# A two-layer hybrid encoder on one core: GpSimd's tensor work goes to the vector and scalar engines, and the MLP norm's factor, squared, goes into the last residual add

## The chip, the cores and the metric

One Trainium2 chip, one of its cores. The metric is the device time of one execution in microseconds (us). The engines go by their short names: PE is the tensor engine (matmul), PEld its weight loads, DVE the vector engine, ACT the scalar engine, POOL GpSimd, SP the engine that issues the DMAs.

## The reference, cut to what matters

The program runs two layers over 256 tokens of 1024 features in float32. Each layer normalises, projects to many branches (a gated linear attention, a dilated attention, a differential attention, a "hyena" convolution by Fourier transform), merges them by gates, projects out, and ends with an MLP:

```
for i in range(2):
    h = rmsnorm(x, norm1_g[i])
    ...
    x = x + m @ w_out[i]
    h2 = rmsnorm(x, norm2_g[i])
    x = x + square(relu(h2 @ mlp_w1[i])) @ mlp_w2[i]

rmsnorm(x, g) = x * rsqrt(mean(x*x) + 1e-6) * g
hyena: y = irfft(rfft(z) * rfft(kern)); kern from two filters hf, hb over the sum of their absolute values
       return x0 * (y + z * skip)
```

The factor rsqrt(...) of a token is one positive number r. It passes through the matrix product and the ReLU unchanged, and comes out of the square as r squared, so it may as well be multiplied in at the end, token by token.

## The kernel before, in words

**Tiling.** The 256 tokens are two blocks of 128 (tb 0 and 1). Every float32 factor of a large product is split into a high part `hi` and a remainder `lo`, and each product is three matmuls (`mm3`, lines 241 to 243: hi by hi, hi by lo, lo by hi). Weights come as `raw` tiles by DMA from SP; `split_to` (line 210 on) makes their `hi` on ACT (line 222) and their `lo = raw - hi` on DVE (line 224), up to four halves of a unit ahead of use. Products whose output has tokens on the partitions go through `chunk_tm`: 128x512 matmuls into two PSUM tiles, one for each token block, either with the blocks side by side or, with `tb_major`, first all of block 0 and then all of block 1. `hooks={(tb, q): f}` calls `f` ahead of quarter `q` of block `tb`. Products with features on the partitions go through `unit_fm` with 128x256 matmuls.

**What POOL does.** While `self.relief` is set, `split_to` gives every second `lo` to POOL (line 223). It is set at three kinds of places: before the first layer's input projections, in `out_proj` when half of the `wo1` product is done, and in the last products of an MLP that another layer follows. POOL also does the four sums of the hyena filters (lines 572 to 581), four of the twelve products and sums that multiply two spectra, and the difference PO of the two results (lines 900 to 907), and it scales z by the skip gain (line 914). Besides, it does the reciprocal root of every norm (`rstd`, lines 302 and 303: an add, then a power of -0.5), on 1 to 8 numbers of each partition.

**Order of the work.** The attention and hyena branches are generators. `tick` runs between groups of matmuls. It lets every generator in `evq` take one step, and one in `mixq` if the credit (1.4 for a tick, up to 3.0) is positive; what a step yields is taken off the credit. So the numbers that a generator yields place its matmuls among the large products. All engines run their instructions in the order written.

**Around the change.** `out_proj` runs `wo0` (output columns 0 to 511), then `wo1` (columns 512 to 1023, `tb_major`). After each, `residual` adds PSUM to x on DVE (line 359) and `square` sums x squared on ACT (line 355). `norm_scale(tb)` takes the sum on POOL (line 364), `rstd` on POOL, and makes `xn = x * r * g` in two halves on DVE (line 375), with g broadcast to all partitions by a 512 KB load. `norm_trans(tb)` transposes xn on PE (line 310) and splits the result into `hi` on ACT (line 317) and `lo` on DVE (line 318), tile name `act`. The first product of the MLP, `m1b` (also `tb_major`), needs these. For block 0 both are hooked into `wo1`'s second half; for block 1 `norm_scale` follows `wo1` and `norm_trans` is hooked into `m1b`.

Of the kernel before, what the change touches and what calls it, by code (L numbers as in the profile page):

```python
# [14 lines left out]
ALU = mybir.AluOpType  # L15
# [106 lines left out]
class Kern:  # L122
    def __init__(self, ctx, tc, a):
# [17 lines left out]
        self.evq, self.mixq = [], []  # L141
        self.relief = False
        self.credit = 0.0
# [198 lines left out]

    def load_gain(self, g=None):
        self.gt = None
        if g is not None:
            t = self.t4([128, D], "g")
# [9 lines left out]

    def residual(self, tb, c, p, o=0, n=512):
        xs = self.x[tb][:, c * 512 + o:c * 512 + o + n]
        self.nc.vector.tensor_add(xs, xs, p)

# [15 lines left out]

    def norm_trans(self, tb):
        t = slice(tb * 128, tb * 128 + 128)
        for c in range(2):
            p = self.transposes([self.xn[c][:, j * 128:(j + 1) * 128] for j in range(4)])  # L380
            hi, lo = [self.hpair[i][c][:, :, t] for i in range(2)]
            if self.gt is not None:
                self.split(hi, lo, p)
                continue
            gs = [self.gcol[:, 4 * c + j:4 * c + j + 1] for j in range(4)]
            for j in range(4):
                self.nc.scalar.activation(hi[:, j].bitcast(F32R), p[:, j], AF.Identity, scale=gs[j])
            for j in range(4):
                self.nc.vector.scalar_tensor_tensor(lo[:, j].bitcast(F32R), p[:, j], gs[j], hi[:, j], ALU.mult, ALU.subtract)

# [6 lines left out]
    def setup(self):  # L397
# [133 lines left out]
    def filters(self, p):  # L531
# [43 lines left out]
        ab = [self.t4([128, 2, 512], "ab") for _ in range(2)]  # L575
        nc.scalar.activation(ab[0], hf, AF.Abs)
        nc.scalar.activation(ab[1], hb, AF.Abs)
        yield 0.0
        nc.gpsimd.tensor_add(ab[0], ab[0], ab[1])
        yield 0.0  # L580
        nc.gpsimd.tensor_add(ab[0][:, 0], ab[0][:, 0], ab[0][:, 1])
        p.K = [self.t4([128, 2, 512], "K") for _ in range(2)]
# [11 lines left out]
        for cb in range(4):  # L594
            nc.tensor.matmul(ps[:, cb:cb + 1], lhsT=ab[0][:, 0, cb * 128:(cb + 1) * 128], rhs=self.one, start=True, stop=True)
        p.invn = self.cp.tile([128, 4], F32, tag=f"invn{l}", name=self.nm("invn"))
# [6 lines left out]
    def gla_in(self, act, p):  # L603
# [8 lines left out]
        self.chunk_tm("gr", act, ev_r, tb_major=True, hooks={(1, 0) if self.l else (0, 3): lambda: self.norm_trans(1)})  # L612
        self.relief = False
        st.v1, lr = self.t2([128, 2, 256], "dv1"), self.t2([128, 2, 32], "lr")
# [257 lines left out]
    def hyena(self, st, p):  # L872
# [177 lines left out]

    def out_proj(self, gain):
        act = self.views(self.mpair)
        self.load_gain(gain)

# [8 lines left out]
        def mid():  # L1063
            self.relief = True
            self.norm_scale(0)

        self.chunk_tm("wo1", act, ev(1), tb_major=True, hooks={(1, 0): mid, (1, 3): lambda: self.norm_trans(0)})
        self.norm_scale(1)
        return self.views(self.hpair)

    def mlp(self, act, last):
# [16 lines left out]
        def first():  # L1088
# [18 lines left out]
            g = []  # L1107
            self.chunk_tm("m1b", act, ev, tb_major=True, hooks={(1, 0): lambda: self.norm_trans(1)})
            self.relief = False
            for j in range(2):  # L1110
# [23 lines left out]
        ws = [self.take(f"m2.{j}", k, ahead=False) for j in (14, 15) for k in range(2)]  # L1134
        self.relief = not last
        for tb in range(2):
            for c in range(2):
# [6 lines left out]
                if last:  # L1144
                    n = 256 if tb and c else 512
                    for o in range(0, 512, n):
                        self.residual(tb, c, acc[tb][c][:, o:o + n], o, n)
                        cc = slice(c * 512 + o, c * 512 + o + n)
                        nc.sync.dma_start(self.a["out"][tb * 128:(tb + 1) * 128, cc], self.x[tb][:, cc])
                elif tb == 0:  # L1150
                    self.residual(tb, c, acc[tb][c])
                    self.square(tb, c)
            if tb == 0 and not last:
                self.norm_scale(0)
        if not last:
            for c in range(2):
                self.residual(1, c, acc[1][c])
                self.square(1, c)
            self.norm_scale(1)

    def run(self):
# [11 lines left out]
        self.norm_scale(1)  # L1173
        self.relief = True
        p = self.params(0)
        self.evq += [p.derive, self.filters(p)]
        for l in range(L):
# [67 lines left out]
def lay_out(inputs):  # L1245
# [11 lines left out]
    for l in range(L):  # L1257
# [10 lines left out]
        for i, k in enumerate(("hy_b1", "hy_freq1", "hy_b2", "hy_freq2")):  # L1268
# [28 lines left out]
```

## Time and profile before

| | |
|---|---|
| time, median of 3 runs | 1133.13 us (1133.01 to 1134.49) |
| the profiled execution: own time | 1133.93 us |
| the profiled execution: span from first to last instruction | 1132.1 us |
| busy: PE, DVE, ACT, POOL | 97%, 65%, 51%, 14% of the span |
| granted clock of PE, mean | 0.990 |
| DMA | 196.87 MB, mean 174 GB/s |

Times in the trace count from the first instruction. A matmul's shown duration is modelled and overlaps the next; how fast PE runs is read from the distance between starts. Idle time of an engine stands in brackets behind a row, with what ended it.

### The profile page before, as it was taken

What the parts mean: (1) busy time and instruction counts of PE and PEld (TensorE: products, weight loads), DVE (VectorE), ACT (ScalarE), POOL (GpSimd) and SP (SyncE); (2) the same over time, 40 slices, a digit from 0 to 9 for tenths busy, and PEclk for the clock granted to TensorE, in tenths of its full rate; (3) what the DMA queues carried; (4) which work ended last, traced back from release to release, by engine and by line L of the source; (5) the groups of instructions that cost most, each with busy time, mean ns of one, the idle gap of its engine ahead of it and who ended that gap; (6) DMA issues with size and microseconds to landing.
All of it is one profiled execution on the core that took longest, in us unless ns stands there. A gap on an engine that the chain in (4) does not pass through costs nothing. (4 is left out here: it accounts for less than half of the span.)

```text
span 1132.1 us, 17927 instructions
## 1 busy us (share of the span) xinstructions
PE 1100.9 (97%) x7374; PEld 983.4 (87%) x7374; DVE 734.5 (65%) x993; ACT 575.3 (51%) x870; POOL 156.5 (14%) x124
## 2 busy tenths in 40 slices
PE   7999989999999899999999999899999998999998
PEld 5889778999999688899878997789999996989997
DVE  5787776658567667755555777676486665555644
ACT  6854535555444356444547555445463454454542
POOL 2031362000000210300030014530010003100000
PEclk9999999999999999999999999999999998999999
DMA  8434445743464554445435444366534653545452
GB/s 306 174 134 150 167 150 157 216 165 134 150 223 172 190 198 179 166 177 223 156 135 217 149 159 158 145 177 184 202 112 149 223 205 112 217 160 218 180 192 75
DMA packets 41527, 196.87 MB, mean 174 GB/s; under 512 B 4770, under 2 KB 15939, under 8 KB 20197
## 3 DMA queue, kind: packets, MB, share of 16 engines
q1 hardware_dynamic: 41444, 195.72, 48.9%
q8 instruction: 58, 0.95, 0.3%
q14 instruction: 25, 0.20, 0.1%
HBM read 194.62 MB, written 1.08 MB: 173 GB/s over the span
## 5 line engine op out<-in xcount | busy, mean ns | idle before, releaser
L224 DVE TENSOR_TENSOR lo<-raw,hi 128x1024 fp32r<-128x1024 f32 x338 | 423.4, 1272 | 132.6 <-ACT hi L222 132.0
L241 PE MATMUL w<-act,hi 128*128 128x256 f32 x1440 | 407.1, 283 | 0.0
L242 PE MATMUL w<-act,hi 128*128 128x256 f32 x1440 | 401.1, 279 | 0.0
L243 PE MATMUL w<-act,lo 128*128 128x256 f32 x1440 | 401.0, 278 | 0.0
L222 ACT CAST hi<-raw 128x1024 fp32r<-128x1024 f32 (+2 forms) x352 | 349.4, 1031 | 39.3 <-ACT hi L222 14.1
L241 PEld LDWEIGHTS w<-act,hi 128*128 128x128 f32 x1440 | 272.2, 189 | 7.9 <-issue 3.3
L242 PEld LDWEIGHTS w<-act,hi 128*128 128x128 f32 x1440 | 270.9, 188 | 1.6 <-issue 0.2
L243 PEld LDWEIGHTS w<-act,lo 128*128 128x128 f32 x1440 | 271.0, 188 | 0.0
L243 PE MATMUL w<-hi,act 128*128 128x512 f32 (+1 forms) x416 | 164.0, 394 | 9.3 <-DVE act L318 9.2
L241 PE MATMUL w<-hi,act 128*128 128x512 f32 (+1 forms) x416 | 168.7, 405 | 1.9 <-ACT act L317 0.9
L242 PE MATMUL w<-lo,act 128*128 128x512 f32 (+1 forms) x416 | 163.8, 394 | 3.3 <-DVE lo L224 3.3
L243 PEld LDWEIGHTS w<-hi,act 128*128 128x128 f32 x416 | 81.0, 195 | 27.8 <-DVE act L318 11.6
L242 PEld LDWEIGHTS w<-lo,act 128*128 128x128 f32 x416 | 81.1, 195 | 20.5 <-DVE lo L224 5.3
L241 PEld LDWEIGHTS w<-hi,act 128*128 128x128 f32 x416 | 81.3, 195 | 19.6 <-issue 1.7
L243 PE MATMUL acc<-hi,u 128*128 128x512 f32 x224 | 88.3, 394 | 0.0
L242 PE MATMUL acc<-lo,u 128*128 128x512 f32 x224 | 87.8, 392 | 0.0
L241 PE MATMUL acc<-hi,u 128*128 128x512 f32 x224 | 87.5, 391 | 0.0
L1081 DVE TENSOR_TENSOR u<-u 128x512 f32<-128x512 f32 x28 | 20.0, 715 | 85.6 <-ACT u L1079 85.6
L1079 ACT ACTIVATE u<-w 128x512 f32<-128x512 f32 x28 | 16.7, 598 | 114.3 <-PE w L243 114.3
L1033 ACT ACTIVATE sg<-w 128x512 f32<-128x512 f32 x32 | 19.1, 597 | 93.4 <-PE w L243 93.4
L302 POOL TENSOR_SCALAR s<-s 128x8 f32<-128x8 f32 (+2 forms) x36 | 10.2, 283 | 358.9 <-DVE s L737 357.1
L303 POOL TENSOR_TENSOR s<-s,mhalf 128x8 f32<-128x8 f32 (+2 forms) x36 | 55.0, 1528 | 3.0
(227 smaller groups left out, 1095.4 us busy)
## 6 DMA issues: line engine op xcount, KB each, us to landing
raw<-in_w SPq DMA_DIRECT2D x166, 1024.0 KB, 4.9
raw<-in_w SPq DMA_DIRECT2D x8, 512.0 KB, 3.3
raw<-in_w SPq DMA_DIRECT2D x4, 576.0 KB, 3.7
b<-bias SPq DMA_DIRECT2D x32, 64.0 KB, 6.3
b<-bias SPq DMA_DIRECT2D x16, 128.0 KB, 7.4
b<-bias SPq DMA_DIRECT2D x8, 256.0 KB, 5.9
g<-in_n SPq DMA_DIRECT2D x3, 512.0 KB, 5.8
w<-in_hw SPq DMA_DIRECT2D x2, 512.0 KB, 6.3
```

The source lines that it names most:

```text
L222: nc.scalar.copy(hi.bitcast(F32R), src)
L224: eng.tensor_sub(lo.bitcast(F32R), src, hi)
L241: mm(out, lhsT=lh, rhs=rh, start=start, stop=False)
L242: mm(out, lhsT=lh, rhs=rl, start=False, stop=False)
L243: mm(out, lhsT=ll, rhs=rh, start=False, stop=stop)
L302: self.nc.gpsimd.tensor_scalar(x, ss, inv, EPS, ALU.mult, ALU.add)
L303: self.nc.gpsimd.tensor_tensor(y, x, self.mhalf[:, 0:n], ALU.pow)
L1033: self.unit_fm(f"gate_{b}.{2 * i + j}", act, lambda _, ps: nc.scalar.activation(sg[:, 2 * j:2 * j + 2], ps, AF.Tanh, scale=0.5))
L1079: nc.scalar.activation(r, ps, AF.Relu)
L1081: nc.vector.tensor_mul(sq, r, r)
```

## The change

It takes the tensor work off POOL and leaves it the `rstd` numbers. The `lo` parts are always made on DVE; the filters' sums, the spectra's sums and PO go to DVE, the scaling of z to ACT, and the yields of those steps grow. The MLP's norm is no longer applied ahead of the product: x itself is transposed, the gain of each feature (now on partitions) is multiplied in as `hi` and `lo` are made, in pieces of 128x128 (`gain_trans`), and r squared (`inv_ms`, three small DVE instructions for each block, no power) is a factor of the last residual add. The broadcast gain load becomes a load of 128x8. `r2t` takes 128 bytes of each partition, so that every tile allocated behind it lies 128 bytes further on; the offset of activations to weights within 128 bytes, which is 64, stays.

```diff
-            eng = nc.gpsimd if self.relief and self.hi_ % 2 else nc.vector
-            eng.tensor_sub(lo.bitcast(F32R), src, hi)
+            nc.vector.tensor_sub(lo.bitcast(F32R), src, hi)
...
-    def residual(self, tb, c, p, o=0, n=512):
+    def residual(self, tb, c, p, o=0, n=512, scale=None):
...
+        if scale is None:
+            self.nc.vector.tensor_add(xs, xs, p)
+        else:
+            self.nc.vector.scalar_tensor_tensor(xs, p, scale, xs, ALU.mult, ALU.add)
...
+    def gain_trans(self, tb, c, src, gain=True):
+        t = slice(tb * 128, tb * 128 + 128)
+        p = self.transposes([src[:, j * 128:(j + 1) * 128] for j in range(4)])
+        hi, lo = [self.hpair[i][c][:, :, t] for i in range(2)]
+        if not gain:
+            self.split(hi, lo, p)
+            return
+        gs = [self.gcol[:, 4 * c + j:4 * c + j + 1] for j in range(4)]
+        for j in range(4):
+            self.nc.scalar.activation(hi[:, j].bitcast(F32R), p[:, j], AF.Identity, scale=gs[j])
+        for j in range(4):
+            self.nc.vector.scalar_tensor_tensor(lo[:, j].bitcast(F32R), p[:, j], gs[j], hi[:, j], ALU.mult, ALU.subtract)
+
+    def inv_ms(self, tb):
+        s = self.r2t[:, tb:tb + 1]
+        nc.vector.tensor_scalar(s, self.ss[tb][:, 0:1], self.ss[tb][:, 1:2], 1.0 / D, ALU.add, ALU.mult)
+        nc.vector.tensor_scalar_add(s, s, EPS)
+        nc.vector.reciprocal(s, s)
+        return s
...
+        self.r2t = cp.tile([128, 32], F32, name="r2t")
...
-        nc.gpsimd.tensor_add(hs, hf, hb)
-        nc.gpsimd.tensor_sub(hd, hf, hb)
-        yield 0.5
...
-        nc.gpsimd.tensor_add(ab[0], ab[0], ab[1])
-        yield 0.0
-        nc.gpsimd.tensor_add(ab[0][:, 0], ab[0][:, 0], ab[0][:, 1])
+        nc.vector.tensor_add(hs, hf, hb)
+        yield 1.2
+        nc.vector.tensor_sub(hd, hf, hb)
+        yield 1.2
+        nc.vector.tensor_add(ab, ab, ab2)
+        yield 1.2
+        nc.vector.tensor_add(ab[:, 0], ab[:, 0], ab[:, 1])
+        yield 0.6
...
-            nc.gpsimd.tensor_sub(Y[:, 0], Y[:, 0], a)
-            yield 1.2
+            nc.vector.tensor_sub(Y[:, 0], Y[:, 0], a)
+            yield 1.9
...
-            nc.gpsimd.tensor_add(Y[:, 1], Y[:, 1], b)
-            yield 1.2
+            nc.vector.tensor_add(Y[:, 1], Y[:, 1], b)
+            yield 1.9
...
-        nc.gpsimd.tensor_sub(PO, pr[0], pr[1])
         nc.vector.tensor_add(PE, pr[0], pr[1])
         yield 1.1
+        nc.vector.tensor_sub(PO, pr[0], pr[1])
+        yield 1.1
...
-            nc.gpsimd.tensor_scalar(z[:, cb], z[:, cb], p.par[:, 10 + cb:11 + cb], None, ALU.mult)
+            nc.scalar.activation(z[:, cb], z[:, cb], AF.Copy, scale=p.par[:, 10 + cb:11 + cb])
...
-        self.chunk_tm("wo1", act, ev(1), tb_major=True, hooks={(1, 0): mid, (1, 3): lambda: self.norm_trans(0)})
-        self.norm_scale(1)
+        self.chunk_tm("wo1", act, ev(1), tb_major=True, hooks={
+            (0, 2): lambda: self.gain_trans(0, 0, xs(0, 0)), (1, 0): mid, (1, 2): lambda: self.gain_trans(0, 1, xs(0, 1))})
+        self.last_trans = lambda: self.gain_trans(1, 1, xs(1, 1))
...
-            self.chunk_tm("m1b", act, ev, tb_major=True, hooks={(1, 0): lambda: self.norm_trans(1)})
-            self.relief = False
+            self.chunk_tm("m1b", act, ev, tb_major=True, hooks={(0, 2): self.last_trans})
+            self.r2 = [self.inv_ms(tb) for tb in range(2)]
...
-                    self.residual(tb, c, acc[tb][c])
+                    self.residual(tb, c, acc[tb][c], scale=self.r2[tb])
```

In the new `out_proj`, `mid` is `gain_trans(1, 0, xs(1, 0))`.

How this moves instructions on DVE at the way into the first layer's MLP, where x_86 and x_87 are the two token blocks of x. Before, from block 0's residual add of `wo1` on:

```order
L359 TENSOR_TENSOR x_86<-x_86,w_4003 128x512
L375 SCALAR_TENSOR_TENSOR xn_4042<-x_86,s_4039,g_3919 128x512
L375 SCALAR_TENSOR_TENSOR xn_4043<-x_86,s_4039,g_3919 128x512
L224 TENSOR_TENSOR lo_4053<-raw_3949,hi_4052 128x1024
L224 TENSOR_TENSOR lo_4069<-raw_3983,hi_4068 128x1024
L318 TENSOR_TENSOR act_3925<-tp_4084,act_3923 128x4x128
L318 TENSOR_TENSOR act_3926<-tp_4091,act_3924 128x4x128
L359 TENSOR_TENSOR x_87<-x_87,w_4004 128x512
```

Now, from the same residual add of block 0 to that of block 1 and the last piece:

```order
L361 TENSOR_TENSOR x_86<-x_86,w_4004 128x512
L397 SCALAR_TENSOR_TENSOR act_3926<-tp_4050,gcol_3920,act_3924 128x128 x4
L222 TENSOR_TENSOR lo_4070<-raw_3950,hi_4069 128x1024
L222 TENSOR_TENSOR lo_4076<-raw_3950,hi_4075 128x1024
L222 TENSOR_TENSOR lo_4086<-raw_3984,hi_4085 128x1024
L397 SCALAR_TENSOR_TENSOR act_3927<-tp_4091,gcol_3920,act_3925 128x128 x4
L222 TENSOR_TENSOR lo_4111<-raw_3984,hi_4110 128x1024
L361 TENSOR_TENSOR x_87<-x_87,w_4005 128x512
L222 TENSOR_TENSOR lo_4124<-raw_4073,hi_4123 128x1024
L397 SCALAR_TENSOR_TENSOR act_3927<-tp_4159,gcol_3920,act_3925 128x128 x4
```

The xn products are gone, the activations' `lo` pieces stand earlier, and block 1's last residual add now has four weight `lo` parts and two groups of pieces ahead of it. Its result is what the transposes hooked into `m1b` read.

And DVE in the first layer's hyena branch, from the second spectrum's last products to PE's first product with P. Before:

```order
L902 TENSOR_TENSOR Y_1467<-Z_1401,K_742 128x512
L903 TENSOR_TENSOR u_1533<-Z_1401,K_742 128x512
L224 TENSOR_TENSOR lo_1573<-raw_1414,hi_1572 128x1024
L908 TENSOR_TENSOR P_1588<-Y_1466,Y_1467 128x1024
L224 TENSOR_TENSOR lo_1593<-raw_1477,hi_1592 128x1024
L737 TENSOR_REDUCE s_1612<-u_1610 128x8
L737 TENSOR_REDUCE s_1620<-u_1618 128x8
```

Now:

```order
L920 TENSOR_TENSOR Y_1468<-Z_1402,K_800 128x512
L921 TENSOR_TENSOR u_1566<-Z_1402,K_800 128x512
L922 TENSOR_TENSOR Y_1468<-Y_1468,u_1566 128x512
L222 TENSOR_TENSOR lo_1590<-raw_1478,hi_1589 128x1024
L755 TENSOR_REDUCE s_1609<-u_1607 128x8
L755 TENSOR_REDUCE s_1617<-u_1615 128x8
L222 TENSOR_TENSOR lo_1628<-raw_1478,hi_1627 128x1024
L765 TENSOR_TENSOR u_1643<-w_1511,s_1612 128x512
L765 TENSOR_TENSOR u_1645<-w_1512,s_1620 128x512
L222 TENSOR_TENSOR lo_1648<-raw_1537,hi_1647 128x1024
L925 TENSOR_TENSOR P_1679<-Y_1467,Y_1468 128x1024
L222 TENSOR_TENSOR lo_1683<-raw_1537,hi_1682 128x1024
```

The norm's reductions and products (lines 755 and 765) now stand ahead of the P sums, where before they stood behind P, and PE's products with P stand 48 large matmuls later than before.

## Rows read from the trace of the kernel before

**Rows 1.** The page, part 1: busy time, share of the span, instructions.

```profile
PE 1100.9 (97%) x7374; PEld 983.4 (87%) x7374; DVE 734.5 (65%) x993; ACT 575.3 (51%) x870; POOL 156.5 (14%) x124
```

**Rows 2.** Stretches: us from:to, length, busy PE, PEld, DVE, ACT, POOL, clock, DMA.

```profile
150.00:166.00 16.00, 12.37 (x57) 10.32 (x56) 11.62 (x12) 5.85 (x9) 12.31 (x10) 0.89 0.37 132
...
708.50:724.00 15.50, 11.88 (x55) 9.76 (x54) 11.25 (x12) 6.04 (x9) 13.40 (x10) 0.89 0.37 135
...
945.73:952.57 6.84, 4.61 (x11) 3.68 (x12) 5.12 (x6) 1.66 (x3) 1.44 (x4) 0.50 0.76 287
...
396.00:560.00 164.00, 163.71 (x1051) 145.95 (x1050) 103.77 (x117) 81.19 (x101) 16.29 (x6) 1.00 0.50 188
```

**Rows 3.** Timeline of PE, into the first layer's MLP: start, us, instruction, [idle before].

```profile
383.67 0.39 PE L241 MATMUL w<-hi,act 128*128 128x512 f32 x1
384.87 0.50 PE L242 MATMUL w<-lo,act 128*128 128x512 f32 x1 [0.81 <-DVE lo L224]
388.76 0.50 PE L243 MATMUL w<-hi,act 128*128 128x512 f32 x1 [3.39 <-DVE act L318]
...
392.96 0.40 PE L242 MATMUL w<-lo,act 128*128 128x512 f32 x1
```

**Rows 4.** Timeline of PE, the same place in the second layer.

```profile
942.17 0.40 PE L241 MATMUL w<-hi,act 128*128 128x512 f32 x1
...
942.86 0.39 PE L241 MATMUL w<-hi,act 128*128 128x512 f32 x1
...
952.71 0.40 PE L242 MATMUL w<-lo,act 128*128 128x512 f32 x1
```

**Rows 5.** Timelines of DVE, POOL and ACT, into the first layer's MLP.

```profile
377.40 0.69 DVE L359 TENSOR_TENSOR x<-x,w 128x512 f32<-128x512 f32 x1 [1.95 <-PE w L243]
380.07 1.41 DVE L375 SCALAR_TENSOR_TENSOR xn<-x,s,g 128x512 f32<-128x512 f32 x2 [1.98 <-POOL s L303]
381.40 6.71 DVE L224 TENSOR_TENSOR lo<-raw,hi 128x1024 fp32r<-128x1024 f32 x2
...
380.82 6.20 POOL L224 TENSOR_TENSOR lo<-raw,hi 128x1024 fp32r<-128x1024 f32 x2 [0.79 <-DVE xn L375]
...
378.13 0.63 ACT L355 ACTIVATE junk<-x 128x512 f32<-128x512 f32 x1 [3.94 <-DVE x L359]
...
378.76 3.96 ACT L222 CAST hi<-raw 128x1024 fp32r<-128x1024 f32 x4
```

**Rows 6.** Timeline of PE in the first layer's hyena branch.

```profile
154.32 0.71 PE L921 MATMUL p<-dfti,P 128*128 128x128 f32 x4 [1.36 <-POOL P L907]
...
158.74 0.66 PE L310 MATMUL tp<-ident,u 128*128 128x128 f32 x4 [0.92 <-DVE u L747]
```

**Rows 7.** Timelines of POOL and DVE in the first layer's hyena branch.

```profile
150.87 3.39 POOL L907 TENSOR_TENSOR P<-Y,Y 128x1024 f32<-128x1024 f32 x1
...
156.31 1.65 POOL L303 TENSOR_TENSOR s<-s,mhalf 128x8 f32<-128x8 f32 x1
...
151.97 3.38 DVE L224 TENSOR_TENSOR lo<-raw,hi 128x1024 fp32r<-128x1024 f32 x1
...
156.46 1.21 DVE L224 TENSOR_TENSOR lo<-raw,hi 128x1024 fp32r<-128x1024 f32 x1
```

**Rows 8.** Timelines of PE and DVE from the first layer into the second.

```profile
580.04 0.50 PE L243 MATMUL w<-hi,act 128*128 128x512 f32 x1 [2.40 <-DVE act L318]
...
576.35 3.03 DVE L224 TENSOR_TENSOR lo<-raw,hi 128x1024 fp32r<-128x1024 f32 x1 [0.31 <-ACT hi L222]
...
580.50 1.72 DVE L224 TENSOR_TENSOR lo<-raw,hi 128x576 fp32r<-128x576 f32 x1
...
585.40 1.41 DVE L375 SCALAR_TENSOR_TENSOR xn<-x,s,g 128x512 f32<-128x512 f32 x2 [1.98 <-POOL s L303]
```

**Rows 9.** Timeline of DVE: instructions of one kind back to back.

```profile
562.80 3.50 DVE L224 TENSOR_TENSOR lo<-raw,hi 128x1024 fp32r<-128x1024 f32 x3 [0.26 <-ACT hi L222]
...
9.79 2.15 DVE L389 SCALAR_TENSOR_TENSOR act<-tp,gcol,act 128x128 fp32r<-128x128 f32 x8
```

More of the change, by code (lines that the diff above doesn't have):

```diff
@@ L340, in views, with load_gain @@
         return self.View(pair[0], n), self.View(pair[1], n)
-    def load_gain(self, g=None):
+    def load_gain(self, g=None, gcol=None):
         self.gt = None
+        if gcol is not None:
+            self.gcol = self.ts([128, 8], "gcol")
+            self.nc.sync.dma_start(self.gcol, gcol)
         if g is not None:
@@ L377, in norm_trans @@
     def norm_trans(self, tb):
+        for c in range(2):
+            self.gain_trans(tb, c, self.xn[c], self.gt is None)
+    def gain_trans(self, tb, c, src, gain=True):
         t = slice(tb * 128, tb * 128 + 128)
[L379 to L389, printed above, removed]
+        p = self.transposes([src[:, j * 128:(j + 1) * 128] for j in range(4)])
[9 more added lines that the diff above has]
+    def inv_ms(self, tb):
+        nc = self.nc
+        s = self.r2t[:, tb:tb + 1]
[3 more added lines that the diff above has]
+        return s
     def load_const(self, name, shape, alloc=None):
@@ L571, in filters @@
         hs, hd = self.t4([128, 2, 512], "hs"), self.t4([128, 2, 512], "hd")
-        nc.gpsimd.tensor_add(hs, hf, hb)
-        nc.gpsimd.tensor_sub(hd, hf, hb)
-        yield 0.5
-        ab = [self.t4([128, 2, 512], "ab") for _ in range(2)]
-        nc.scalar.activation(ab[0], hf, AF.Abs)
-        nc.scalar.activation(ab[1], hb, AF.Abs)
-        yield 0.0
-        nc.gpsimd.tensor_add(ab[0], ab[0], ab[1])
-        yield 0.0
-        nc.gpsimd.tensor_add(ab[0][:, 0], ab[0][:, 0], ab[0][:, 1])
+        ab, ab2 = [self.t4([128, 2, 512], "ab") for _ in range(2)]
+        nc.scalar.activation(ab, hf, AF.Abs)
+        nc.scalar.activation(ab2, hb, AF.Abs)
+        nc.vector.tensor_add(hs, hf, hb)
[6 more added lines that the diff above has]
+        yield 0.6
         p.K = [self.t4([128, 2, 512], "K") for _ in range(2)]
@@ L594, in filters @@
         for cb in range(4):
-            nc.tensor.matmul(ps[:, cb:cb + 1], lhsT=ab[0][:, 0, cb * 128:(cb + 1) * 128], rhs=self.one, start=True, stop=True)
+            nc.tensor.matmul(ps[:, cb:cb + 1], lhsT=ab[:, 0, cb * 128:(cb + 1) * 128], rhs=self.one, start=True, stop=True)
         p.invn = self.cp.tile([128, 4], F32, tag=f"invn{l}", name=self.nm("invn"))
@@ L612, in gla_in @@
         self.chunk_tm("gr", act, ev_r, tb_major=True, hooks={(1, 0) if self.l else (0, 3): lambda: self.norm_trans(1)})
-        self.relief = False
         st.v1, lr = self.t2([128, 2, 256], "dv1"), self.t2([128, 2, 32], "lr")
@@ L1049, in merge, with out_proj @@
             self.unit_fm(f"proj_{b}.{i}", y, ev)
-    def out_proj(self, gain):
+    def out_proj(self):
         act = self.views(self.mpair)
-        self.load_gain(gain)
+        self.load_gain(gcol=self.a["n2c"][self.l])
+        xs = lambda tb, c: self.x[tb][:, c * 512:(c + 1) * 512]
         def ev(c):
@@ L1063, in mid @@
         def mid():
-            self.relief = True
-            self.norm_scale(0)
-        self.chunk_tm("wo1", act, ev(1), tb_major=True, hooks={(1, 0): mid, (1, 3): lambda: self.norm_trans(0)})
-        self.norm_scale(1)
+            self.gain_trans(1, 0, xs(1, 0))
+        self.chunk_tm("wo1", act, ev(1), tb_major=True, hooks={
+            (0, 2): lambda: self.gain_trans(0, 0, xs(0, 0)), (1, 0): mid, (1, 2): lambda: self.gain_trans(0, 1, xs(0, 1))})
+        self.last_trans = lambda: self.gain_trans(1, 1, xs(1, 1))
         return self.views(self.hpair)
@@ L1134, in mlp @@
         ws = [self.take(f"m2.{j}", k, ahead=False) for j in (14, 15) for k in range(2)]
-        self.relief = not last
         for tb in range(2):
@@ L1146, in mlp @@
                     for o in range(0, 512, n):
-                        self.residual(tb, c, acc[tb][c][:, o:o + n], o, n)
+                        self.residual(tb, c, acc[tb][c][:, o:o + n], o, n, self.r2[tb])
                         cc = slice(c * 512 + o, c * 512 + o + n)
@@ L1156, in mlp @@
             for c in range(2):
-                self.residual(1, c, acc[1][c])
+                self.residual(1, c, acc[1][c], scale=self.r2[1])
                 self.square(1, c)
@@ L1173, in run @@
         self.norm_scale(1)
-        self.relief = True
         p = self.params(0)
@@ L1190, in run @@
             self.merge("c", act, gc, yc, last=True)
-            act = self.out_proj(self.a["n2"][l:l + 1, :])
+            act = self.out_proj()
             if not last:
@@ L1276, in lay_out @@
     arrays = {"w": w, "x": c(x["x"].reshape(S, D)), "t5": c(x["t5_bias"]), "par": par, "gw": gw, "hw12": hw12,
-              "hw3": c(np.concatenate([x["hy_w3"]] * 2, axis=1)), "n1": c(x["norm1_g"]), "n2": c(x["norm2_g"]),
+              "hw3": c(np.concatenate([x["hy_w3"]] * 2, axis=1)), "n1": c(x["norm1_g"]), "n2c": c(x["norm2_g"].reshape(L, 8, 128).transpose(0, 2, 1)),
               "gcol": c(x["norm1_g"][0].reshape(8, 128).T),
```

2 lines of the change are left out of this document (removed).

## Prediction

> **What bounds the kernel now.** I read the page's busy shares first, then the distances between PE's starts, then the waits, each followed to the instruction that was late. PE is busy for 1100.9 of 1132.1 us [rows 1], so the kernel is PE-bound, and only what lets PE stand still or run at half clock can be won. A large 128x512 matmul starts every 0.23 us (942.17 to 942.86 is three of them) [rows 4]. Stretches in which PE keeps that pace have nothing to give: from 396 to 560 it is busy for 163.71 of 164.00 us, with DVE at 103.77 and ACT at 81.19 [rows 2]. The loss sits in three kinds of places.
>
> *The way into the MLP.* In the first layer 13 steps of 0.23 us, 2.99 us of work, take from 383.67 to 392.96, 9.29 us: 6.3 us lost [rows 3]. PE waits 0.81 us for a weight `lo` and 3.39 us for the activations' `lo` (line 318), and after that starts come slower. DVE's row shows why: two `lo` of 128x1024 take 6.71 us beside POOL's two, 6.20 us [rows 5], where three in a row took 3.50 us elsewhere, 1.14 us for each after the first [rows 9]. The activations' `lo` stands behind them. In the second layer the same 13 steps take from 942.86 to 952.71, so 6.9 us are lost; most of that stretch, 6.84 us, runs at a granted clock of 0.50, which is 1.2 GHz [rows 2, 4].
>
> *The hyena branch.* PE is idle for 16.00 - 12.37 = 3.6 us in the first layer and for 15.50 - 11.88 = 3.6 us in the second, and at a mean granted clock of 0.89 gives away another 0.11 x 16 = 1.8 and 0.11 x 15.5 = 1.7 us [rows 2]: 10.7 us for both. The waits are named: 1.36 us for P on POOL, then for u on DVE, 0.92 us and another like it [rows 6]. PO takes POOL 3.39 us, and the DVE `lo` beside it, ahead of the norm's reductions, 3.38 us [rows 7].
>
> *From one layer to the next.* PE waits 2.40 us for the same kind of `lo` [rows 8], and goes on at half clock as in the other places.
>
> **The change, part by part.** All sums go against the profiled execution's own time, 1133.9 us, 0.8 us above the median of 1133.1.
>
> *Way into the MLP.* Gone from the chain are the power on POOL, the products xn (1.41 us, begun 1.98 us late for POOL) and POOL's `lo`; the activations' `lo` pieces now stand ahead of the weight `lo`. I take DVE's `lo` at 1.14 us [rows 9]. A new wait arises: the transposes hooked into `m1b` need block 1's residual add, which stands on DVE behind four weight `lo` and two groups of pieces, and everything on PE queues behind the transposes. Let T be the end of block 0's `wo1` on PE. The first pieces need the residual, 0.69, and on ACT the square, 0.63 [rows 5], and four `hi` pieces, for which I take the 2.15/8 = 0.27 us of DVE's pieces of that shape [rows 9], 1.08: with the handovers T + 2.6. From there DVE has 1.08 + 3 x 1.14 + 1.08 + 1.14 + 0.69 = 7.4 us of work, and ends at T + 10.0. PE has the 24 matmuls of block 1, 5.6, eight transposes, about 0.8, and the 12 matmuls of two quarters of `m1b`, 2.8, and is there at T + 9.2. With the handover PE waits 0.9 us. Low end: no wait, if DVE gets its first `hi` sooner. High end: 2 us, if ACT's four weight `hi`, 3.96 us in a row [rows 5], get ahead of pieces, and then half clock for 3.4 us as in the hyena stretch, 1.6 us lost. I take 0.9, as the counted instructions give it, and no half clock: after the 0.81 us wait alone PE's start distances did not grow; that came after the 3.39 [rows 3]. Gain 6.3 + 6.9 - 2 x 0.9 = **11.4 us**, between 6.0 and 13.2.
>
> *Hyena branch.* DVE takes over two sums of 128x512 for each spectrum, about 0.69 each as the residual of that shape [rows 5], and PO, about 1.2: 4.0 us in each layer. In return its `lo` there stop being stretched, by 2.2 us beside PO alone [rows 7]; DVE is busy for 11.62 of 16.00 us [rows 2], so even without that return it fits. The reductions of the norm now stand ahead of P, and P's products on PE come 48 matmuls, 11 us, later, so the 3.38 us `lo` and the wait for P leave PE's path. The two powers of the norm stay (1.65 us each) [rows 7] and can still be late: I leave 0.3 us for each layer, between nothing and the 0.92 us of the wait that is left of this kind [rows 6]. No half clock without the long waits. Gain 10.7 - 0.6 = **10.1 us**, between 8.9 and 10.7.
>
> *The powers that stay on POOL.* A DVE `lo` that ran inside such a power, 156.46 beside 156.31, took 1.21 us [rows 7], as one alone, so I take nothing for them. The Trainium skill, page "SBUF — State Buffer", section "SBUF: two separate sides", says otherwise: the port pair that DVE and GpSimd share is a lock, and a DVE instruction with two SBUF inputs that comes second is fully blocked until the GpSimd one ends. By that the sum would be smaller by the third rival's price; the trace does not agree, since the lo was not held up.
>
> *From layer to layer.* DVE's two `lo` there shrink from 3.03 and 1.72 us to 1.2 and, for 576 columns, some 0.7, which frees 2.8 us, and two of POOL's come over, 2.3 us [rows 8, 9]. What follows is block 1's residual, square, power and xn at 585.40, for which PE would next stand still [rows 8]. So **0.5 us** stays of it; the high end is the whole wait and half clock, 2.4 + 1.7 = 4.1, if that chain moves up as well, the low end 0.
>
> *At nothing.* The filters' sums on DVE, three of 1.2 and one of 0.7 us in a layer, lie beside stretches in which DVE is idle for 60 of 164 us and PE is not [rows 2]; without that cover they would cost at most 4.3 us a layer. The scaling of z goes to an ACT that is busy for 5.85 of 16 us [rows 2]. `inv_ms` is six instructions on one number a partition, a whole MLP ahead of its use. The factor in the last residual is one more operand, and only the last of these adds stands at the program's end; I take nothing. The smaller gain load starts ahead of `wo0` and nobody waited for the larger one. The 128 bytes of `r2t` keep every tile's offset to the weights within 128; a change of PE's pace by 1% would be 10 us either way, and I see no row for one.
>
> **Sum.** 11.4 + 10.1 + 0.5 = 22.0 us; 1133.9 - 22.0 = 1111.9, and 0.8 less for the median: **1111 us**. With the terms' usual errors the forecast's own range is 1107 to 1115.
>
> **The rivals.**
>
> 1. *The new wait in `m1b` is long* and is followed by half clock: 2 + 1.6 instead of 0.9 us in each layer, 5.4 us, 1116.5. For it: the hook's slack is negative by my own count, and DVE holds seven instructions in front. Against: none of them need be stretched now. Chance 0.17.
> 2. *DVE becomes late in the hyena branch*: it takes over 4.0 us, and P's sums and the norm's products stand in one queue with weight `lo` that must keep up. A wait of 3 us with half clock, 4.5 instead of 0.3, makes 8.4 us for two layers: 1119.5. Against: DVE's 11.62 of 16 us, and the yields grow, which puts the steps further apart. Chance 0.09.
> 3. *The powers block DVE*: each holds up the `lo` beside it by its 1.65 us, and PE behind it, with half clock 1.7: 2 x 3.4 = 6.7 us in two layers, 1118. It is what the Trainium skill's rule above would do here. Against: the 1.21 us [rows 7]. Chance 0.05.
> 4. *Everything goes*: no new wait, no rest in the hyena branch, and the layer boundary moves up: 13.2 + 10.7 + 4.1 = 28.0, 1105. Chance 0.06.
> 5. *Slower: DVE is what stretches its own `lo`*, by its traffic with ACT and the DMAs at these places, not POOL. Then the four `lo` ahead of block 1's residual take 3.36 us each instead of 1.14, DVE ends 8.9 us later, and PE waits 9.8 us with half clock 1.7, against the 6.6 lost now: 4.9 x 2 = 10 us slower; the hyena branch gains nothing and the boundary neither: 1143. It decides from about 2.2 us for a `lo` there, where 0.9 + 4 x 1.1 + 1.6 passes 6.6. Against: 1.21 us beside POOL's light power, 3.38 beside its heavy sum, a microsecond or so apart [rows 7]. Chance 0.03.
> 6. *It does nothing in sum*: the waits return one place further on, or the pace changes by the amount won. 1131 to 1135. Chance 0.04.
>
> **How the numbers follow.** The forecast keeps 0.56. The likeliest time is 1111. The range reaches from rival 4 to rival 2, 1104 to 1120, and leaves out rivals 5 and 6 with 0.07 and the tails of the others. A measurement of this kernel can tell 0.2%, 2.3 us, from no change: forecast and rivals 1 to 4 are faster by more, 0.93; rival 6 is the same, 0.04; rival 5 slower, 0.03.
>
> **What would show it.** POOL's 156.5 us fall to less than half, with no row of 128x512 or more left, and DVE's `lo` are all near 1.2 us. On the way into the MLP the waits for the activations' `lo` (line 318, then 397) are gone, PE shows one wait of about 1 us in `m1b` for block 1's x, and the clock stays at 1.00. In the hyena branch the wait for P is gone. At the boundary a wait of 2 to 4 us remains, ahead of the transposes of xn instead. I am wrong if DVE's `lo` stay near 3 us, if PE's waits in `m1b` pass 2 us, or if 128x256 matmuls change their pace.

## The result, and the profile after

| | before | changed |
|---|---|---|
| time, median of 4 runs each | 1133.07 us (1132.56 to 1134.49) | 1119.88 us (1119.67 to 1120.35) |
| ratio to before, 95% interval | | 0.9882 [0.9865, 0.9899] |
| span of the profiled execution | 1132.1 us | 1117.9 us |
| granted clock of PE, mean | 0.990 | 0.999 |
| busy PE / idle PE in the span | 1100.9 / 31.2 us | 1100.9 / 17.0 us |

The change makes the kernel 13.2 us faster, at the slow end of the range, 1120, and far from the 1111 that was forecast. The page of the changed kernel, parts 1 and 2 (the clock's row in tenths, in 40 slices), answers to [rows 1]:

```profile
PE 1100.9 (98%) x7374; PEld 983.6 (88%) x7374; DVE 729.9 (65%) x1053; ACT 582.0 (52%) x902; POOL 65.5 (6%) x72
...
PEclk9999999999999999999999999999999999999999
```

POOL fell from 156.5 to 65.5 us. The granted clock's row is all nines (before, one slice read 8). That is odd beside the first number: PE is busy for 1100.9 us in both kernels, with the same 7374 matmuls, although before some of them ran at half clock. Something must have made the others longer. First the places that the forecast named.

**The way into the first MLP**, the timeline of PE, answers to [rows 3]:

```profile
380.33 0.39 PE L239 MATMUL w<-hi,act 128*128 128x512 f32 x1
...
382.90 0.40 PE L241 MATMUL w<-hi,act 128*128 128x512 f32 x1
...
383.92 0.66 PE L308 MATMUL tp<-ident,x 128*128 128x128 f32 x4 [0.62 <-DVE x L361]
...
384.33 0.48 PE L239 MATMUL w<-hi,act 128*128 128x512 f32 x1
```

380.33 is the first matmul of `m1b`. From there 12 steps and the four transposes (0.41 us) take 4.00 us; before, 13 steps from the same matmul took 9.29 [rows 3]. One wait is left, 0.62 us for block 1's residual, where 0.9 was forecast. It is the same in the second layer, 0.62 us at 934.96. DVE's timeline shows the queue that was counted out:

```profile
376.56 1.13 DVE L397 SCALAR_TENSOR_TENSOR act<-tp,gcol,act 128x128 fp32r<-128x128 f32 x4 [1.82 <-ACT act L395]
377.61 3.49 DVE L222 TENSOR_TENSOR lo<-raw,hi 128x1024 fp32r<-128x1024 f32 x3
381.01 1.12 DVE L397 SCALAR_TENSOR_TENSOR act<-tp,gcol,act 128x128 fp32r<-128x128 f32 x4
382.05 1.22 DVE L222 TENSOR_TENSOR lo<-raw,hi 128x1024 fp32r<-128x1024 f32 x1
383.18 0.68 DVE L361 TENSOR_TENSOR x<-x,w 128x512 f32<-128x512 f32 x1
```

Pieces, three `lo` in 3.49 us, pieces, a `lo`, and the residual last: from 376.56 to 383.86 it is 7.3 us of unbroken work, forecast 7.4.

**The hyena branch** of the first layer, PE's timeline, answers to [rows 6]:

```profile
145.56 0.66 PE L308 MATMUL tp<-ident,u 128*128 128x128 f32 x4 [0.96 <-DVE u L765]
...
158.15 0.66 PE L308 MATMUL tp<-ident,u 128*128 128x128 f32 x4 [0.45 <-DVE u L765]
```

The wait for P is gone, and so is the half clock. Two waits for u are left, 0.96 and 0.45 us, more than the 0.3 that was forecast. The timelines of DVE, then POOL, tell why; they answer to [rows 7]:

```profile
142.07 1.22 DVE L222 TENSOR_TENSOR lo<-raw,hi 128x1024 fp32r<-128x1024 f32 x1
...
144.81 0.69 DVE L765 TENSOR_TENSOR u<-w,s 128x512 f32<-128x512 f32 x1 [0.93 <-POOL s L301]
...
153.88 1.22 DVE L222 TENSOR_TENSOR lo<-raw,hi 128x1024 fp32r<-128x1024 f32 x1
...
157.40 0.69 DVE L765 TENSOR_TENSOR u<-w,s 128x512 f32<-128x512 f32 x1 [1.31 <-POOL s L301]
...
142.29 2.49 POOL L301 TENSOR_TENSOR s<-s,mhalf 128x8 f32<-128x8 f32 x1
...
153.73 1.64 POOL L301 TENSOR_TENSOR s<-s,mhalf 128x8 f32<-128x8 f32 x1
```

DVE's `lo` take 1.22 us. What is late is the norm's power on POOL: for one of 2.49 us, where others take 1.64, DVE's u waits 0.93 us, and for a later one of the usual length 1.31 us.

**From one layer to the next**, PE's timeline, answers to [rows 8]:

```profile
572.81 0.50 PE L241 MATMUL w<-hi,act 128*128 128x512 f32 x1 [1.30 <-DVE act L316]
...
579.36 0.63 PE L308 MATMUL tp<-ident,xn 128*128 128x128 f32 x4 [1.16 <-DVE xn L379]
```

The 2.40 us for the activations' `lo` are now 1.30, the half clock behind it is gone, and a new wait, 1.16 us for xn, stands where the forecast put it.

**Where the rest went.** So the waits shrank as forecast, or nearly. But look at stretches in which PE never waits. The view of stretches (length, busy PE, PEld, DVE, ACT, POOL, clock, DMA) of the kernel before, then of the changed one; 960 to 1080 lies within the last MLP in both:

```profile
300.00:350.00 50.00, 50.00 (x427) 50.00 (x426) 30.10 (x34) 21.25 (x28) 0.00 (x0) 1.00 0.49 180
...
960.00:1080.00 120.00, 120.00 (x794) 109.41 (x793) 67.69 (x65) 57.72 (x69) 5.00 (x2) 1.00 0.52 193
```

```profile
300.00:350.00 50.00, 50.00 (x427) 50.00 (x426) 31.96 (x35) 23.47 (x30) 0.00 (x0) 1.00 0.53 190
...
960.00:1080.00 120.00, 120.00 (x762) 107.81 (x761) 65.14 (x65) 55.27 (x65) 0.00 (x0) 1.00 0.48 181
```

PE is busy for 120.00 of 120.00 us at clock 1.00 in both, and gets through 794 matmuls before and 762 now, 4% fewer. The timeline of PE in the first MLP, a run of 128x256 matmuls, in the kernel before and in the changed one: the two rows of each are the same two instructions of the program, 22 matmuls apart.

```profile
501.56 0.28 PE L242 MATMUL w<-act,hi 128*128 128x256 f32 x1
...
504.05 0.28 PE L243 MATMUL w<-act,lo 128*128 128x256 f32 x1
```

```profile
493.52 0.28 PE L240 MATMUL w<-act,hi 128*128 128x256 f32 x1
...
496.12 0.28 PE L241 MATMUL w<-act,lo 128*128 128x256 f32 x1
```

2.49 us against 2.60: one starts every 113 ns before and every 118 ns now. The duration shown, 0.28, is the same: it is modelled, and hides this. And the trace of before had both paces in it: its stretch from 300 to 350, a run of 128x256 matmuls as well, does 427 in 50 us, 117 ns each, and does so still.

### The profile page after: what moved, and what is told of

Its sections match the earlier page's. It is cut to its first block, busy times and chain, and to the rows that moved or that the text cites. A ratio compares the mean times of both kernels' runs of the same rounds, so it can differ in the third digit from the quotient of the medians.

```text
span 1117.9 us, 17949 instructions
## 1 busy us (share of the span) xinstructions
PE 1100.9 (98%) x7374; PEld 983.6 (88%) x7374; DVE 729.9 (65%) x1053; ACT 582.0 (52%) x902; POOL 65.5 (6%) x72
## 3 DMA queue, kind: packets, MB, share of 16 engines
HBM read 193.58 MB, written 1.08 MB: 174 GB/s over the span
## 4 chain that ended last, share of the span: by engine, by line
PE 91%; DVE 4%; POOL 2%; issue 1%; DMA 1%; ACT 1%; SPq 0%; DVEq 0%; ACTq 0%; POOLq 0%
PE w L239 22%; PE w L241 22%; PE w L240 21%; PE acc L241 5%; PE acc L239 5%; PE acc L240 5%; PE tp L308 3%; DVE lo L222 2%; POOL s L301 1%; DMA raw<-in_w 1%; PE p L816 1%; PE p L846 1%; PE p L940 1%; PE p L1020 1%; PE p L905 1%
## 5 line engine op out<-in xcount | busy, mean ns | idle before, releaser
L222 DVE TENSOR_TENSOR lo<-raw,hi 128x1024 fp32r<-128x1024 f32 (+2 forms) x352 | 414.6, 1198 | 140.2 <-ACT hi L221 139.1
L221 ACT CAST hi<-raw 128x1024 fp32r<-128x1024 f32 (+2 forms) x352 | 349.1, 1031 | 31.2 <-ACT hi L221 15.5
L239 PE MATMUL w<-hi,act 128*128 128x512 f32 (+1 forms) x416 | 165.9, 399 | 1.5 <-ACT act L395 1.2
L240 PE MATMUL w<-lo,act 128*128 128x512 f32 (+1 forms) x416 | 161.4, 388 | 1.4 <-DVE lo L222 1.4
L241 PE MATMUL w<-hi,act 128*128 128x512 f32 (+1 forms) x416 | 161.3, 388 | 1.3 <-DVE act L316 1.3
L239 PEld LDWEIGHTS w<-hi,act 128*128 128x128 f32 x416 | 79.4, 191 | 18.4 <-issue 1.7
L241 PEld LDWEIGHTS w<-hi,act 128*128 128x128 f32 x416 | 79.4, 191 | 18.3 <-DVE act L316 2.2
L241 PEld LDWEIGHTS acc<-hi,u 128*128 128x128 f32 x224 | 41.9, 187 | 10.4
```

Source lines behind the costliest of these rows:

```text
L222: nc.vector.tensor_sub(lo.bitcast(F32R), src, hi)
L239: mm(out, lhsT=lh, rhs=rh, start=start, stop=False)
L240: mm(out, lhsT=lh, rhs=rl, start=False, stop=False)
L241: mm(out, lhsT=ll, rhs=rh, start=False, stop=stop)
```

## The experiments

**1. What sets the pace.** By the order and sizes of the tiles, the program's allocation puts the weights' `hi` and `lo` at 128 within each 256 bytes of a partition, and before the change put the activations at 64; no trace shows an address, and what the runs test is the moves. The 128 bytes of `r2t` moved them to 192. Within 128 bytes nothing changed; within 256 bytes the place did.

```diff
-        self.r2t = cp.tile([128, 32], F32, name="r2t")
+        self.r2t = cp.tile([128, 64], F32, name="r2t")
```

> The changed kernel with r2t of 256 bytes a partition instead of 128; nothing else. In the changed kernel all waits and half-clock stretches together fell by about 22 us as forecast, but the time by 13 only, and in both MLPs a 128x256 matmul starts every 117.6 ns, where it was 113.4 before, and a 128x512 one every 233.3 instead of 228.8. Theory A, the place of the activations in SBUF sets the pace: the weights lie at 128 within 256 bytes, the activations lay at 64 before and lie at 192 now; with 256 bytes they are back at 64, the pace goes back to about 113.5 ns in both MLPs and the time falls by 8 us, to 1111 or 1112. Theory B, the pace is a state that PE falls into by the timing of what comes before, and the place has nothing to do with it: pace 117.6 ns and 1119.9 us, as changed.

1106.61 us, ratio to before 0.9761 [0.9747, 0.9776], that is 13.3 us less than the changed kernel. Part 1 of its page, and the stretch in the last MLP:

```profile
PE 1088.3 (98%) x7374; PEld 976.3 (88%) x7374; DVE 729.7 (66%) x1053; ACT 582.3 (53%) x902; POOL 65.4 (6%) x72
```

```profile
960.00:1080.00 120.00, 120.00 (x789) 109.16 (x789) 66.63 (x67) 56.43 (x66) 0.00 (x0) 1.00 0.51 191
```

PE's busy time fell from 1100.9 to 1088.3 us, idle time stayed (16.6 after 17.0), and the stretch holds 789 matmuls again. Theory A holds. The gain was larger than expected, since the slow pace had not been in the MLPs alone: PE reaches the transposes of x in the first MLP at 381.21 us instead of 383.92, and only 0.5 of these 2.7 us are shorter waits.

The other way round, the kernel before with nothing but 128 bytes in that place:

```diff
+        pad = cp.tile([128, 32], F32, name="pad")
+        nc.vector.memset(pad, 0.0)
         nc.vector.memset(self.mhalf, -0.5)
```

> The kernel before, with an unused tile of 128 bytes a partition where the change puts r2t; nothing else moves. Theory A (place): the activations go from 64 to 192 within 256 bytes, 128x256 matmuls in the MLPs go from 113.4 to about 117.6 ns, and the time rises by about 8 us, to 1141. Theory B (state of PE): pace and time as before, 1133.

1144.73 us, 1.0091 [1.0067, 1.0115] of before, 10.7 us more. In the last MLP:

```profile
960.00:1080.00 120.00, 120.00 (x766) 107.88 (x765) 66.30 (x65) 58.12 (x69) 5.27 (x2) 1.00 0.48 181
```

No engine's work or order changed but for one memset at the start, and PE does 766 matmuls where it did 794. That an unused tile costs 10 us is the clearest run of this study.

Two further sizes of `r2t`, 64 and 192 bytes (`[128, 16]` and `[128, 48]`):

> The changed kernel with r2t of 64 bytes: activations at 128 within 256 bytes, the same as the weights. Theory A: a third pace; the words of the change, that activations stand 64 bytes off the weights, suggest that this is the worse place, so 117.6 ns or more and 1120 to 1135 us. Theory B: as changed, 1119.9.

> The changed kernel with r2t of 192 bytes: activations at 0 within 256 bytes, weights at 128. So far, at 64: 128x256 every 113.4 ns in the MLPs, 1106.6 us; at 128: 120 ns, 1123.1; at 192: 117.6 ns, 1119.9. If the pace is set by the distance of the activations from the weights within 256 bytes in either direction (64 and 192 are 64 off on either side and yet differ), 0 should lie with 192 or 64; if it is set by the place of the activations alone, it has a value of its own. I expect between 1106 and 1120 us, and no change in any wait.

1123.08 us (0.9905 [0.9889, 0.9922]) and 1125.28 us (0.9940 [0.9923, 0.9958]). Their last MLPs, first with 64 bytes, then with 192:

```profile
960.00:1080.00 120.00, 120.00 (x779) 110.05 (x778) 64.34 (x64) 53.22 (x63) 0.00 (x0) 1.00 0.51 193
```

```profile
960.00:1080.00 120.00, 120.00 (x767) 108.90 (x766) 65.72 (x64) 54.10 (x63) 0.00 (x0) 1.00 0.50 189
```

Both are slow, though the stretch with 64 bytes holds 779 matmuls, between the two paces. PE's timeline there, first two rows of a run of 128x256 matmuls, 40 apart, then two of a run of 128x512, 20 apart, shows why:

```profile
960.75 0.28 PE L241 MATMUL w<-act,lo 128*128 128x256 f32 x1
...
965.55 0.28 PE L239 MATMUL w<-act,hi 128*128 128x256 f32 x1
...
966.61 0.40 PE L239 MATMUL acc<-hi,h 128*128 128x512 f32 x1
...
971.15 0.39 PE L241 MATMUL acc<-hi,lo 128*128 128x512 f32 x1
```

A 128x256 matmul starts every 120 ns, slower than in any kernel so far, and a 128x512 one every 227, a little faster than the 228.8 ns of the kernel before. The two shapes don't have the same best place, so a count over both can mislead. My guess that the place 0 (`r2t` of 192 bytes) would give 1106 to 1120 was wrong: it is the slowest of the four.

Is it the place of the activations, or their distance from the weights? `r2t` in a pool ahead of all others moves both:

```diff
+        self.fp = P("fp", 1)
         self.wp = P("wp", NRAW)
...
-        self.r2t = cp.tile([128, 32], F32, name="r2t")
+        self.r2t = self.fp.tile([128, 32], F32, name="r2t")
```

> The changed kernel with r2t, 128 bytes as in the change, in a pool of its own ahead of all others, so that weights and activations move by it alike: the activations lie at 192 within 256 bytes as in the change, the weights go from 128 to 0, and the distance between them is again the one of before. If the distance from the weights sets the pace: 113.4 ns for 128x256 and 1106.6 us. If the place of the activations alone does: 117.6 ns and 1119.9 us.

1106.85 us, 0.9766 [0.9744, 0.9788]:

```profile
960.00:1080.00 120.00, 120.00 (x791) 109.26 (x790) 66.61 (x66) 56.40 (x66) 0.00 (x0) 1.00 0.51 192
```

In the MLPs it is the distance. All runs together, places within 256 bytes, distance of the activations (and of all else behind `r2t`) from the weights; the kernel before stands at its own level:

| kernel | weights | activations | distance | matmuls, 960 to 1080 | us |
|---|---|---|---|---|---|
| before | 128 | 64 | -64 | 794 | 1133.1 |
| before, 128 bytes put in | 128 | 192 | +64 | 766 | 1144.7 |
| changed | 128 | 192 | +64 | 762 | 1119.9 |
| r2t of 256 bytes | 128 | 64 | -64 | 789 | 1106.6 |
| r2t ahead of all | 0 | 192 | -64 (192 - 256) | 791 | 1106.9 |
| r2t of 64 bytes | 128 | 128 | 0 | 779 | 1123.1 |
| r2t of 192 bytes | 128 | 0 | 128 | 767 | 1125.3 |

The stretches begin at slightly different places of the product, so their counts compare to about 1%.

The distance isn't all of it. In the second layer's gate products, all 128x256, the view of stretches gives for the kernel before, then for the same with 128 bytes put in:

```profile
870.00:900.00 30.00, 30.00 (x257) 30.00 (x256) 19.40 (x21) 13.29 (x17) 0.00 (x0) 1.00 0.60 211
```

```profile
870.00:900.00 30.00, 30.00 (x267) 30.00 (x266) 19.48 (x22) 13.19 (x17) 0.00 (x0) 1.00 0.57 199
```

Here +64 is the faster: 100 steps take 11.33 us, and the same 100 in the kernel before 11.78. The changed kernel, at +64 too, does 257 there, and in the first layer's gate products (300 to 350) both distances give 427. What decides in these products was not found.

**2. Whether POOL's `lo` were the cause at the MLP.** The changed kernel with every second `lo` on POOL again, on the way into each MLP only (8 `lo`; the kernel before gave POOL 14). The expectation speaks of three places, but the edit sets `relief` in `out_proj` alone:

```diff
-            nc.vector.tensor_sub(lo.bitcast(F32R), src, hi)
+            eng = nc.gpsimd if self.relief and self.hi_ % 2 else nc.vector
+            eng.tensor_sub(lo.bitcast(F32R), src, hi)
```

> The changed kernel with every second weight lo given to POOL again in the three places of before; filters, spectra and z stay off POOL, the norm's factor stays at the end. My theory, POOL's lo stretches DVE's: DVE's lo beside them take 3.0 to 3.4 us instead of 1.2, block 1's residual comes some 2 us later, PE's wait at the hook in m1b grows from 0.8 to about 3 us and is followed by half clock, 1.6 us; with a little at the start and at the layer boundary the time rises by 7 to 12 us, to 1127 to 1132. Rival, DVE stretches its own lo by its traffic at these places: DVE has two lo fewer there, they take 1.2 us, and the time is the same or a little less, 1117 to 1120.

1119.96 us, as the changed kernel's 1119.88. Timelines of DVE (three rows), POOL and PE on the way into the first MLP:

```profile
378.39 1.22 DVE L224 TENSOR_TENSOR lo<-raw,hi 128x1024 fp32r<-128x1024 f32 x1
...
380.17 2.77 DVE L224 TENSOR_TENSOR lo<-raw,hi 128x1024 fp32r<-128x1024 f32 x1 [0.57 <-ACT hi L222]
...
383.91 0.67 DVE L363 TENSOR_TENSOR x<-x,w 128x512 f32<-128x512 f32 x1
...
379.27 2.59 POOL L224 TENSOR_TENSOR lo<-raw,hi 128x1024 fp32r<-128x1024 f32 x1 [80.58 <-ACT hi L222]
...
384.63 0.66 PE L310 MATMUL tp<-ident,x 128*128 128x128 f32 x4 [0.56 <-DVE x L363]
```

My expectation was wrong, and so was the rival's reason. DVE's `lo` beside POOL's is stretched, 2.77 us against 1.22, so that part of the theory holds. But POOL takes two of the four `lo`, so DVE is done with its queue no later: PE waits 0.56 us here, 0.62 with all `lo` on DVE. DVE's `lo` ends 1.08 us after POOL's, and a `lo` alone takes 1.14 [rows 9]: it looks held up until POOL's was done, and not slowed throughout. The delay is real and costs nothing where it stands. The start of the program and the layer boundary were not tested.

**3. The three parts alone**, each in the kernel before, with the activations at the good distance. The norm's factor at the end and the new order, POOL kept busy (the change without its lines on `lo`, filters, spectra and z, and with `r2t` of 256 bytes), cut to the lines that decide:

```diff
-        self.chunk_tm("wo1", act, ev(1), tb_major=True, hooks={(1, 0): mid, (1, 3): lambda: self.norm_trans(0)})
-        self.norm_scale(1)
+        self.chunk_tm("wo1", act, ev(1), tb_major=True, hooks={
+            (0, 2): lambda: self.gain_trans(0, 0, xs(0, 0)), (1, 0): mid, (1, 2): lambda: self.gain_trans(0, 1, xs(0, 1))})
...
-                    self.residual(tb, c, acc[tb][c])
+                    self.residual(tb, c, acc[tb][c], scale=self.r2[tb])
```

> The kernel before with only the norm's factor moved to the end (the transposes of x itself, the order of DVE that goes with it), r2t at 256 bytes so that the activations stay at 64; POOL keeps every second lo at its three places, the filters, the spectra and z. By the run that gave POOL its lo back, the order is what counts at the way into the MLP: gain of about 12 us, nothing in the hyena branch, 1121. By my forecast's reason (DVE's lo stretched by POOL's must go as well): the residual of block 1 comes late, PE waits 3 us with half clock at the hook in each layer, gain about 4 us, 1129.

1118.86 us, 0.9880 [0.9861, 0.9898], 14.0 less, 2 more than expected. In the first layer's hyena branch of the profiled execution the clock was 1.00, though the waits stayed (last section); whether that is the 2 us isn't shown. PE's timeline at the hook has one wait, and none for `act`:

```profile
386.14 0.66 PE L310 MATMUL tp<-ident,x 128*128 128x128 f32 x4 [0.68 <-DVE x L363]
```

The filters, spectra, PO and z alone, those lines of the change with their yields:

```diff
-        nc.gpsimd.tensor_sub(PO, pr[0], pr[1])
         nc.vector.tensor_add(PE, pr[0], pr[1])
         yield 1.1
+        nc.vector.tensor_sub(PO, pr[0], pr[1])
+        yield 1.1
...
```

> The kernel before with only the filters, spectra, PO and z taken off POOL, and their yields; activations stay at 64. Forecast: 10.1 us less, 1123; from the run with r2t of 256 bytes, in which the stretch up to the end of the branches was shorter by 7.1 us in the first layer and 7.7 in the second: 14 to 15 us less, 1119. Rival (DVE gets too full there): 1133 or more.

1121.40 us, 0.9903 [0.9886, 0.9920], 11.5 less: nearer to the forecast's 10.1 than to my later 14 to 15, but above the 10.7 that was its upper bound. Six waits of PE for `sc` (attention), 1.7 us in the kernel before, are gone too, and no term had counted them. The way into the MLP stays as it was, by PE's timeline:

```profile
379.15 0.51 PE L242 MATMUL w<-lo,act 128*128 128x512 f32 x1 [0.82 <-DVE lo L224]
...
383.04 0.50 PE L243 MATMUL w<-hi,act 128*128 128x512 f32 x1 [3.38 <-DVE act L318]
```

The `lo` alone, in the old order:

```diff
-            eng = nc.gpsimd if self.relief and self.hi_ % 2 else nc.vector
-            eng.tensor_sub(lo.bitcast(F32R), src, hi)
+            nc.vector.tensor_sub(lo.bitcast(F32R), src, hi)
```

> The kernel before with only the lo parts taken off POOL, the old order and norm kept, activations at 64. If POOL's lo stretch DVE's and the activations' lo stands behind two of them: DVE makes four lo in 4.6 us where two took 6.7, PE's wait at the way into the MLP is 2 us shorter in each layer, and a little comes at the layer boundary: 1128 to 1129, or 1125 if the half clock goes too. If the stretch costs nothing, because DVE has two lo more to make: 1133.

1123.78 us, 0.9926 [0.9909, 0.9942], 9.1 less, a little better than the good end of what was expected. PE's row, then DVE's:

```profile
386.95 0.50 PE L242 MATMUL w<-hi,act 128*128 128x512 f32 x1 [2.39 <-DVE act L317]
...
381.67 4.62 DVE L223 TENSOR_TENSOR lo<-raw,hi 128x1024 fp32r<-128x1024 f32 x4
...
386.21 1.28 DVE L317 TENSOR_TENSOR act<-tp,act 128x512 fp32r<-128x512 f32 x2
```

Four `lo` take 4.62 us where two took 6.71 [rows 5], so the activations' `lo` come 2.1 us sooner, and PE's two waits, 0.81 and 3.39 us [rows 3], are one of 2.39, with no half clock behind it. The three gains add up to 34.6 us, all parts together give 27.4 (1134.05 to 1106.61): the first and the third both clear the way into the MLP, and it can be cleared but once. How the 7.2 us too many divide between this and the half clock in the hyena branch, which the first two both shorten, was not measured.

**4. The wait that was left.** With `r2t` of 256 bytes, the last transposes one quarter later:

```diff
-            self.chunk_tm("m1b", act, ev, tb_major=True, hooks={(0, 2): self.last_trans})
+            self.chunk_tm("m1b", act, ev, tb_major=True, hooks={(0, 3): self.last_trans})
```

> The changed kernel with r2t of 256 bytes and the last transposes hooked one quarter later into m1b, ahead of the fourth quarter of block 0 instead of the third. PE comes there 6 matmuls, 1.4 us, later, and block 1's residual, now 0.8 to 0.9 us late, is ready. The pieces of it are needed only in the third quarter of block 1, 18 matmuls, 4.2 us, later. If the wait is worth its length: 1.7 us less than with r2t of 256 bytes alone, 1104.9. If it only moves to the pieces or to the next lo: the same, 1106.6.

> The same kernel as the first experiment, on the chip of this call, so that the next hook can be compared with it: 1106.6.

1105.15 us (1104.69 to 1105.25) against 1107.18 (1106.68 to 1107.52), 2.0 less. PE's row at the transposes of x, first with the hook of the change, then one quarter later:

```profile
381.17 0.66 PE L308 MATMUL tp<-ident,x 128*128 128x128 f32 x4 [0.73 <-DVE x L361]
```

```profile
382.25 0.60 PE L308 MATMUL tp<-ident,x 128*128 128x128 f32 x4
```

The wait is gone in both layers, 1.46 us, and from 20 us on the other waits of PE are what they were. (PE's idle time in the span is 16.8 us in both profiles, because the later hook's waited 1.4 us longer in its first 20 us.) This is the fastest version of the study: 0.9751 [0.9732, 0.9769] of before, 27.9 us less.

## Why the prediction was right in its waits and wrong in its sum

*The likeliest time, 1111, was wrong by 9 us, and the step that failed is the term put at nothing for `r2t`.* It said that the 128 bytes of `r2t` keep every tile's offset to the weights within 128, that a change of pace by 1% would be 10 us, and "I see no row for one". The mechanism was named and left without a price in the sum; among the rivals it stands only as a gain that is used up, at 0.04. By the prediction's own last sign, 128x256 matmuls that change their pace, it was wrong. In the MLPs a move of 128 bytes changed the pace and one of 256 gave it back, and the move cost 13.3 us (the changed kernel against `r2t` of 256 bytes). There was a row for it: in the kernel before, 300 to 350 runs at 117 ns for each 128x256 matmul, the first MLP at 113 ns. Two paces at one clock, with no wait in either, say that the pace is something that can be lost, though what separates these two stayed open. The range held the time by luck: it had been drawn for other mishaps, and 1118 to 1119.5 stood there for waits that did not come.

*Way into the MLP: right.* Forecast 11.4 us from 13.2 lost. In the trace PE's wait is 0.6 us in each layer now, so 12.0 were won. The new wait was forecast at 0.9 us and is 0.62. The weight given to POOL's `lo` in it was wrong: with the new order they may stay on POOL at no cost there. The order and the shorter chain of the norm did it. No half clock came, as forecast, but the reason given for that was weak: after the 0.81 us wait one matmul ran before the next wait [rows 3], too few to read a pace from.

*Hyena branch: right, with a rest that was too small.* Forecast 10.1; alone it gave 11.5, 1.7 of it from the waits for `sc`. The waits left are 0.96 and 0.45 us in the first layer where 0.3 was put down. The cause was named, the powers that stay, but not that one of them would take 2.49 us.

*The boundary: mis-sized.* Forecast 0.5; the waits there went from 2.40 us and 1.7 of half clock to 1.30 and 1.16, so 1.6 us. That block 1's chain would be next was right; that its wait would stand there alone, with 2 to 4 us, was not.

*At nothing: right but for `r2t`.* POOL's sums on DVE and z on ACT show in no wait of PE. Sum of the terms as measured: 12.0 + 11.5 + 1.6 = 25.1, against 22.0 forecast and 26 to 27.4 in the three runs with the good distance.

*The rivals.* The long wait in `m1b` (0.17) and a late DVE in the hyena branch (0.09) did not come. That the power blocks a `lo` (0.05) did not come either: the `lo` at 153.88, begun within the power of 153.73, took 1.22 us. It went the other way: the power at 142.29, begun within the `lo` of 142.07, took 2.49 us. The Trainium skill, page "SBUF — State Buffer", section "SBUF: two separate sides", lets whichever starts first of the two block the other; here the second of these pairs fits that and the first does not. Two large ones fit it: the `lo` at 151.97 [rows 7] and the one at 380.17 in the run with POOL's `lo` both ended 1.1 us after POOL's instruction. The slower rival, DVE stretching its own `lo`, is refuted by the run with the `lo` alone: four in 4.62 us with POOL idle. The sixth rival, no change in sum, had the words "the pace changes by the amount won", and they came half true: 13.3 of some 27 us went that way.

## What to carry to other kernels

A new tile, however small, moves all that is allocated behind it: before a change is judged, look whether matmuls of one shape still start at the same distance, by the starts of two far-apart rows and not by the busy share, and try the tile at other sizes. Where a trace shows one shape at two paces with no wait in either, ask what the difference is before counting waits. And two remedies for one stall don't add up: try each alone, since the simpler may be enough.

## What the runs showed that was not expected

- PE's pace in the MLPs depends on the distance of activations and weights in SBUF within 256 bytes, and not alike for each shape: of four distances in steps of 64 bytes, -64 gave 1106.6 us, +64 1119.9, 0 1123.1 and 128 1125.3, with the same instructions and 16.6 to 18.2 us of idle PE in all four. Why, and what sets the pace of the gate products, stays open; finer steps were not tried.
- A wait alone doesn't bring half clock: in the run with the `lo` alone PE waited 2.39 us and went on at full clock, where before it had waited 0.81 and then 3.39 us and fell. In the run with the norm alone, PE's waits in the first layer's hyena branch were 1.35, 0.90 and 1.35 us, in the kernel before 1.36, 0.92 and 1.35; the granted clock of the stretch was 1.00 in the one and 0.89 in the other [rows 2, 6]. In the second layer of that same run the waits were 1.37, 0.90 and 1.35 us and the clock was 0.89.
- A GpSimd power on 8 numbers a partition took 1.64 or 2.49 us, while DVE's `lo` beside it took 1.22 both times.
